# Moving the next expert's token features into the last chunk of the current expert, and reading w2 two consecutive rows to a partition

## The chip, the core and the metric

The kernel runs on one core of a Trainium2 chip. Its time is device microseconds for one execution, the median over several runs. The engines are called as in the profile: PE is TensorE (matmuls and transposes; PEld is its weight load, which overlaps), DVE is VectorE, ACT is ScalarE, POOL is GpSimd, SP is SyncE, which here only issues DMAs.

## What is computed

One block of a transformer on 1024 tokens of width 1024: a token mixer (neighbourhood attention beside a recurrent scan), a layer norm, and then a mixture of 16 experts in which every expert chooses its own 128 tokens. The change touches the experts alone:

```python
aff = softmax(u @ w_router)                      # u: (1024, 1024)
gate, idx = top_k(aff.T, cap)                    # cap = 128 tokens for each of 16 experts
xs = u[idx]                                      # (16, 128, 1024)
hdn = silu(xs @ w1) * (xs @ w3)                  # w1, w3: (16, 1024, 2816)
ye = hdn @ w2 * gate                             # w2: (16, 2816, 1024)
out = zeros.at[idx].add(ye)
```

All of it is float32.

## The kernel before, in words

The mixer takes the first half of the execution, up to about 1628 us; the experts follow, and a last layer norm ends it. The change leaves the mixer's code and the order of its instructions as they are.

**An expert.** Its 2816 hidden columns are cut in three chunks of 1024, 1024 and 768. The steps of the program are written in this order: for each expert e and chunk ci a step (e,ci,1) for w1, a step (e,ci,3) for w3, and then the w2 step of the chunk before it, which for chunk 0 is chunk 2 of expert e-1. A step is cut in units of 256 weight rows: four for w1 or w3, and four, four or three for w2. An expert has 35 units, and this text writes c0w3.1 for chunk 0, w3, unit 1.

**A unit.** `load` asks SP for it 12 units ahead (1 MB, or 768 KB for w1 and w3 of the last chunk; 13 buffers). `split`, two units ahead, makes two float32r halves of it: ACT casts (`hi`, L881), DVE subtracts (`lo`, L882). They share a ring of three buffers each, so `hi` of a unit starts when PE is done with the unit three before it. For each 128 rows PE then runs a pair of matmuls with hi·xh, a pair with lo·xh and a pair with hi·xl, where xh and xl are the halves of the tokens: at L983 into `ph` for w1 and w3, at L998 into `ye` for w2, where the halves of the hidden values (dh, dl) stand for xh and xl.

**Between the steps.** After a w1 step ACT makes silu into `hd` (L986); after w3 DVE multiplies (L988). `hd` is then transposed on PE by 128 columns at a time (L1020) into PSUM tiles named `pt`, from which ACT makes `dh` (L1021) and DVE `dl` (L1022). After the last w2 step of an expert DVE scales `ye` by gate and channel into `yo` (L1003, SCALAR_TENSOR_TENSOR), and POOL scatters it.

**The next expert's tokens.** `prep(e)` makes a one-hot matrix on DVE (L826, 8 instructions), 16 one-column matmuls on PE (L830) into a `pt`, the index of each token on DVE (CAST, L832), and a gather on POOL (L834). `prep2` then makes the features: eight transposes on PE (L846) into two `pt`, eight scale-and-shift copies out of them, four on ACT (L850) and four on DVE (L849), into a tile that is also named `yo`, and from this ACT makes xh (L852, two halves) and DVE xl (L853). `pt` has two buffers, for `prep`, `prep2` and the transposes of `hd` together:

```python
pt=ps_t.tile([128,4,128],F32,name="pt")                     # in prep2, and again for hd
if last and m==1 and ci==1 and e+1<NE: P[e+1]=prep(e+1)
if last and m==2 and ci==0 and e+1<NE: prep2(P[e+1])
```

A scheduler turns this program into one list of instructions for each engine, which the engine runs in order. It may set instructions elsewhere than where the program has them: before the change, from the fourth expert's features on, the eight transposes of `prep2` stand on PE after the last w2 unit of chunk 1, straight ahead of the six transposes of chunk 2's `hd`. The first experts have them earlier.

Of the kernel before, what the change touches and what calls it, by code (L numbers as in the profile page):

```python
# [12 lines left out]
F32 = mybir.dt.float32  # L13
F32R = mybir.dt.float32r
BF16 = mybir.dt.bfloat16
I32 = mybir.dt.int32
# [6 lines left out]
D=1024; T=1024; TC=256; TS=1280; NCT=4  # L23
# [10 lines left out]
NE=16; DE=2816; CAP=128; NT=8  # L34
# [701 lines left out]
def moe(ctx, tc, K, get_t1, mc, i, G, out):  # L736
    nc=tc.nc
    ident,mh,sc2p,sh2=G["ident"],G["mh"],G["sc2p"],G["sh2"]
# [17 lines left out]
    def behind(a,b):  # L756

        tc.add_manual_dep(b.ins,a.ins.name,mybir.DependencyInfo(mybir.DependencyClass.NoSync,mybir.DependencyReason.DATA),reason="order")
# [7 lines left out]
    with ExitStack() as c1:  # L766
        p=c1.enter_context(tc.tile_pool(name="m1",bufs=2,side="right"))
# [5 lines left out]
        for t in range(NT):  # L773
            r=slice(t*128,(t+1)*128)
# [9 lines left out]
            for hh in range(2):  # L784
                pt=ps_t.tile([128,4,128],F32,name="pt")
# [16 lines left out]
            e=p.tile([128,NE],F32,name="ex")  # L802
# [13 lines left out]
    ep=ctx.enter_context(tc.tile_pool(name="ep",bufs=2))  # L816
# [4 lines left out]
    NC_=len(FC)  # L821

    def prep(e):
        oh=ep.tile([128,NT,128],BF16,name="oh",bufs=1)
        for t in range(NT):
            oi=nc.vector.tensor_scalar(oh[:,t,:],iota,slotT[:,t,e:e+1],None,op0=ALU.is_equal)  # L826
            if e in (1,2): behind(P[0]["xi"],oi)
        pi=ps_t.tile([128,4,128],F32,name="pt")
        for t in range(NT):
            for j in range(2): nc.tensor.matmul(pi[:,0,:1],oh[:,t,:],tok[:,t,j:j+1],start=(t+j==0),stop=(t+j==NT))  # L830
        idx=ep.tile([128,1],I32,name="idx")
        ic=nc.vector.tensor_copy(idx,pi[:,0,:1])  # L832
        g=ep.tile([128,D+NE],F32,name="gath",bufs=1)
        gi=nc.gpsimd.indirect_dma_start(out=g,out_offset=None,in_=table[:,:],  # L834
            in_offset=bass.IndirectOffsetOnAxis(ap=idx[:,:1],axis=0))
        return dict(gi=gi,ic=ic,idx=idx,g=g,e=e)

    def prep2(d):
        g=d["g"]; d["gate"]=V[:,0,d["e"]:d["e"]+1]; nc.gpsimd.tensor_copy(d["gate"],g[:,D+d["e"]:D+d["e"]+1])
        xh=ep.tile([128,8,128],F32R,name="xh"); xl=ep.tile([128,8,128],F32R,name="xl")  # L840
        xf=ep.tile([128,8,128],F32,name="yo",bufs=1)
        for hh in range(2):
            pt=ps_t.tile([128,4,128],F32,name="pt")
            for k in range(4):
                kk=hh*4+k
                nc.tensor.transpose(pt[:,k,:],g[:,kk*128:(kk+1)*128],ident)  # L846
            for k in range(4):
                kk=hh*4+k
                if k%2: nc.vector.tensor_scalar(xf[:,kk,:],pt[:,k,:],sc2p[:,kk:kk+1],sh2[:,kk:kk+1],op0=ALU.mult,op1=ALU.add)  # L849
                else: nc.scalar.activation(xf[:,kk,:],pt[:,k,:],AF.Identity,bias=sh2[:,kk:kk+1],scale=sc2p[:,kk:kk+1])  # L850
            c=slice(hh*4,hh*4+4)
            nc.scalar.copy(xh[:,c],xf[:,c])  # L852
            d["xi"]=nc.vector.tensor_sub(xl[:,c],xf[:,c],xh[:,c].bitcast(F32))  # L853
        d["xh"],d["xl"]=xh,xl


    steps=[]
# [8 lines left out]
    def load(u,after=None):  # L866
        z,q=U[u]; e,ci,m=steps[z]; f0,fw=FC[ci]
        if m==2: ap,w=w2[e,f0+q*256:f0+q*256+256,:],D
        else: ap,w=(w1 if m==1 else w3)[e,q*256:q*256+256,f0:f0+fw],fw
        j=len(RN)%(RAW0+RAWB+RAW2); RN.append(0)  # L870
        z=G["raw0"] if j<RAW0 and u<len(U)-FS+LD else raw if j<RAW0+RAWB else raw2
        if len(RN)==1: r=G["r0"]
        else:
            r=z.tile([128,2048],F32,name="raw")
            di=(nc.gpsimd if after else nc.sync).dma_start(r[:,:2*w].rearrange("p (n w) -> p n w",n=2),ap.rearrange("(k p) f -> p k f",p=128))
            if after: behind(after,di)
        SP[u]=(r,w)
    def split(u):
# [6 lines left out]
    with tc.tile_pool(name="m2",bufs=2,side="right") as p:  # L885
# [34 lines left out]
        w=lambda n: p.tile([128,2,128],F32,name=n,bufs=1)  # L920
# [16 lines left out]
        P={0:prep(0)}  # L937
# [5 lines left out]
    def scale_shift(x,nm,rs,op):  # L943
        nc.vector.scalar_tensor_tensor(x,x,nm,g2row,op0=op,op1=ALU.mult)
        nc.vector.scalar_tensor_tensor(x,x,rs,b2row,op0=ALU.mult,op1=ALU.add)
# [25 lines left out]
    for u,(s,q) in enumerate(U):  # L971
        e,ci,m=steps[s]; last=q==nu(ci,m)-1
        for n in range(SN,min(u+LA+1,len(U))): split(n); SN=n+1
        if u+LD<len(U): load(u+LD)
        d=P[e]; w=SP.pop(u); f0,fw=FC[ci]; nf=fw//128
        if m!=2:
            if q==0: PH[m]=[ps_h.tile([128,512],F32,name=f"ph{m}{j}") for j,_ in halves(fw)]
            xh,xl=d["xh"],d["xl"]
            for k in (2*q,2*q+1):
                wh,wl=w[k%2]  # L980
                for x,y,a,b in ((xh,wh,True,False),(xh,wl,False,False),(xl,wh,False,True)):
                    for j,c in halves(fw):
                        nc.tensor.matmul(PH[m][j][:,:c.stop-c.start],x[:,k,:],y[:,c],start=(k==0 and a),stop=(k==7 and b))  # L983
            if last and m==1:
                hd=ep.tile([128,1024],F32,name="hd",bufs=1)
                for j,c in halves(fw): nc.scalar.activation(hd[:,c],PH[1][j][:,:c.stop-c.start],AF.Silu)  # L986
            elif last:
                for j,c in halves(fw): nc.vector.tensor_mul(hd[:,c],hd[:,c],PH[3][j][:,:c.stop-c.start])  # L988
                HD[e,ci]=hd
        else:  # L990
            if ci==0 and q==0: YE[e]=[ps_y.tile([128,512],F32,name=f"ye{j}") for j in range(2)]
            ye=YE[e]; dh,dl=DH[e,ci]
            for k in (2*q,2*q+1):
                st=(ci==0 and k==0); sp=(ci==NC_-1 and k==nf-1)
                wh,wl=w[k%2]
                for l,rr,a,b in ((dh,wh,True,False),(dh,wl,False,False),(dl,wh,False,True)):
                    for j in range(2):
                        nc.tensor.matmul(ye[j],l[:,k,:],rr[:,j*512:(j+1)*512],start=st and a,stop=sp and b)  # L998
            if ci==NC_-1 and last:
                yo=ep.tile([128,D],F32,name="yo",bufs=1)  # L1000
                for j in range(2):
                    c=slice(j*512,(j+1)*512)
                    nc.vector.scalar_tensor_tensor(yo[:,c],ye[j],d["gate"],gt2row[:,c],op0=ALU.mult,op1=ALU.mult)  # L1003
                if e<NE-1:
                    nc.gpsimd.indirect_dma_start(out=acc[:,:],out_offset=bass.IndirectOffsetOnAxis(ap=d["idx"][:,:1],axis=0),  # L1005
                        in_=yo,in_offset=None,compute_op=ALU.add)
                else:
                    nc.vector.tensor_add(yo,yo,ag);
                    nm,rs=ln_stats(nc,None,yo,mh,at=Q[:,0,:16])
                    scale_shift(yo,nm,rs,ALU.subtract)  # L1010

        nxt=steps[s+1] if s+1<len(steps) else None
        for key in list(HD) if last else ():
            if m==2 or (m==3 and (nxt is None or nxt[2]!=2)) or (nxt==(key[0],key[1],2)):
                ee,cc=key; fw2=FC[cc][1]; nf2=fw2//128
                hd=HD.pop(key)
                dh=ep.tile([128,8,128],F32R,name="dh",bufs=1); dl=ep.tile([128,8,128],F32R,name="dl",bufs=1)
                for k0 in range(0,nf2,4):
                    n=min(4,nf2-k0); ks=slice(k0,k0+n); pt=ps_t.tile([128,4,128],F32,name="pt")
                    for k in range(n): nc.tensor.transpose(pt[:,k,:],hd[:,(k0+k)*128:(k0+k+1)*128],ident)  # L1020
                    nc.scalar.copy(dh[:,ks],pt[:,:n])  # L1021
                    nc.vector.tensor_sub(dl[:,ks],pt[:,:n],dh[:,ks].bitcast(F32))  # L1022
                DH[key]=(dh,dl)
        if last and m==1 and ci==1 and e+1<NE: P[e+1]=prep(e+1)
        if last and m==2 and ci==0 and e+1<NE: prep2(P[e+1])
        if u==len(U)-FS:
            ag=ep.tile([128,D+NE],F32,name="gath",bufs=1)[:,:D]
            nc.gpsimd.indirect_dma_start(out=ag,out_offset=None,in_=acc[:,:],in_offset=bass.IndirectOffsetOnAxis(ap=P[NE-1]["idx"][:,:1],axis=0))
            gb=G["raw0"].tile([128,2048],F32,name="raw"); g2row,b2row=gb[:,:D],gb[:,D:]
            for z,n in ((g2row,2),(b2row,3)): nc.sync.dma_start(z,i["lnrows"][n:n+1,:].to_broadcast([128,D]))  # L1030
        for t in range(NT):
            if u==len(U)-XE[t]: final(t)
# [35 lines left out]
```

## Time and profile before

| what | value |
|---|---|
| median of three runs | 3291.5 us (3291.21 to 3293.4) |
| the profiled execution's own time | 3290.45 us |
| its span, first to last instruction | 3288.7 us |
| PE busy / DVE busy / ACT busy / POOL busy | 91% / 72% / 53% / 18% |
| mean granted clock of PE | 0.943 |

The span is 1.75 us under the execution's own time, and that is 1.05 us under the median. Busy shares are means over a mixer and sixteen experts whose limits differ; what the change is worth is read from the experts alone. [...]

### The profile page before, as it was taken

To read this page: it belongs to the slowest core of one execution; us is meant where nothing else is said; L and a number is where in the kernel's file an instruction comes from. 1 tells how busy PE (TensorE), PEld (TensorE's weight loads), DVE (VectorE), ACT (ScalarE), POOL (GpSimd) and SP (SyncE) were. 2 spreads that over 40 slices of the span, in tenths; PEclk is the share of its full clock that TensorE was granted. 3 is DMA by queue.
4 is the path that set the end of the run, shared out by engine and by line. 5 is a ranking of instruction groups with operands and counts; after the bars stand their busy time and mean duration, and the time that the engine had idled before them with its cause. 6 is when DMAs were issued, how large, how long until landed. Compare 5 with 4: busy or idle time off the path is not lost.

```text
span 3288.7 us, 47329 instructions
## 1 busy us (share of the span) xinstructions
PE 3007.9 (91%) x17884; PEld 2392.4 (73%) x17884; DVE 2364.2 (72%) x3206; ACT 1733.2 (53%) x1996; POOL 590.6 (18%) x509
## 2 busy tenths in 40 slices
PE   7999998997888988999699999999999999999995
PEld 4777776776667764677388887787777787777874
DVE  4346445544377678667788998888888988888887
ACT  3343343433134334332277776677666766667665
POOL 2233333333132137120000000000000000000004
PEclk9998999997889989999799999999999999999998
DMA  5345554555777866453789999999999999999975
GB/s 188 90 121 135 126 133 115 136 145 122 170 185 197 195 180 195 136 162 141 275 329 373 370 378 367 346 361 343 341 364 352 365 331 336 359 351 367 335 293 225
DMA packets 537368, 825.17 MB, mean 251 GB/s; under 512 B 206318, under 2 KB 335470, under 8 KB 537012
## 3 DMA queue, kind: packets, MB, share of 16 engines
q1 hardware_dynamic: 489308, 742.36, 66.2%
q10 hardware_dynamic: 42472, 60.25, 5.7%
q0 software_dynamic: 5360, 19.54, 2.3%
q8 instruction: 141, 2.31, 0.3%
q14 instruction: 87, 0.71, 0.1%
HBM read 732.48 MB, written 89.55 MB: 250 GB/s over the span
## 4 chain that ended last, share of the span: by engine, by line
PE 55%; DVE 6%; DMA 5%; ACT 2%; issue 2%; POOL 1%; ACTq 0%; SPq 0%; POOLq 0%; DVEq 0%
PE ph L983 29%; PE ye L998 13%; PE pA L679 3%; PE po L722 2%; DVE lo L882 2%; DMA raw<-in_w_e_dram 2%; PE pt L1020 1%; PE apt L576 1%; PE yp L583 1%; ACT hi L881 1%; PE RY L511 1%; PE RY L508 1%; PE RY L535 1%; PE US L520 1%; DMA vb<-vnD 0%
## 5 line engine op out<-in xcount | busy, mean ns | idle before, releaser
L882 DVE TENSOR_TENSOR lo<-raw,hi 128x2048 fp32r<-128x2048 f32 (+1 forms) x560 | 1199.8, 2170 | 219.4 <-ACT hi L881 202.9
L881 ACT CAST hi<-raw 128x2048 fp32r<-128x2048 f32 (+1 forms) x560 | 1009.8, 1812 | 362.0 <-PE ph L983 228.9
L983 PE MATMUL ph<-hi,xh 128*128 128x512 f32 (+1 forms) x1536 | 460.4, 384 | 3.1 <-ACT xh L852 2.0
L983 PE MATMUL ph<-lo,xh 128*128 128x512 f32 (+1 forms) x1536 | 456.6, 379 | 6.1 <-DVE lo L882 4.6
L983 PE MATMUL ph<-hi,xl 128*128 128x512 f32 (+1 forms) x1536 | 455.4, 378 | 0.4 <-DVE xl L853 0.4
L983 PEld LDWEIGHTS ph<-lo,xh 128*128 128x128 f32 x1536 | 276.6, 192 | 62.1 <-DVE lo L882 6.3
L983 PEld LDWEIGHTS ph<-hi,xh 128*128 128x128 f32 x1536 | 275.8, 193 | 54.8 <-ACT xh L852 2.4
L983 PEld LDWEIGHTS ph<-hi,xl 128*128 128x128 f32 x1536 | 274.4, 191 | 54.0 <-DVE xl L853 1.1
L228 PE MATMUL pp<-uh,whi 128*128 128x512 f32 (+1 forms) x832 | 264.3, 390 | 4.9 <-DVE th L304 3.1
L228 PE MATMUL pp<-ul,whi 128*128 128x512 f32 (+1 forms) x832 | 264.8, 387 | 0.0
L228 PE MATMUL pp<-uh,wlo 128*128 128x512 f32 (+1 forms) x832 | 262.5, 386 | 0.2 <-POOL wlo L216 0.2
L998 PE MATMUL ye<-hi,dh 128*128 128x512 f32 x704 | 221.1, 395 | 1.3 <-ACT dh L1021 1.3
L998 PE MATMUL ye<-lo,dh 128*128 128x512 f32 x704 | 220.7, 395 | 1.7 <-DVE affW L955 1.0
L998 PE MATMUL ye<-hi,dl 128*128 128x512 f32 x704 | 218.4, 391 | 3.2 <-DVE dl L1022 3.2
L1005 POOL DMA_INDIRECT acc<-yo,idx x15 | 24.1, 1604 | 951.8 <-DVE yo L1003 951.8
L228 PEld LDWEIGHTS pp<-uh,whi 128*128 128x128 f32 x832 | 153.5, 195 | 41.2 <-issue 8.2
L228 PEld LDWEIGHTS pp<-uh,wlo 128*128 128x128 f32 x832 | 155.1, 194 | 37.2 <-issue 7.5
L228 PEld LDWEIGHTS pp<-ul,whi 128*128 128x128 f32 x832 | 154.7, 194 | 36.2 <-issue 8.5
L262 DVE TENSOR_TENSOR tmp<-AU,W 120x144 f32<-120x144 f32 (+24 forms) x248 | 93.0, 375 | 116.2 <-DMA AU<-aD 50.1
L998 PEld LDWEIGHTS ye<-hi,dl 128*128 128x128 f32 x704 | 132.6, 188 | 32.3 <-DVE dl L1022 3.6
L998 PEld LDWEIGHTS ye<-lo,dh 128*128 128x128 f32 x704 | 129.3, 188 | 33.9 <-DVE lo L882 8.0
L216 POOL TENSOR_TENSOR wlo<-wraw,whi 128x512 fp32r<-128x512 f32 x86 | 113.3, 1337 | 222.0 <-ACT whi L215 170.8
(331 smaller groups left out, 4480.8 us busy)
## 6 DMA issues: line engine op xcount, KB each, us to landing
raw<-in_w_e_dram SPq DMA_DIRECT2D x430, 1024.0 KB
raw<-in_w_e_dram SPq DMA_DIRECT2D x128, 768.0 KB
wraw<-in_w_in_dram SPq DMA_DIRECT2D x86, 256.0 KB
wmod<-in_w_mod_dram SPq DMA_DIRECT2D x48, 256.0 KB
BTD<-BT SPq DMA_DIRECT2D x40, 256.0 KB
cBT<-BTD SPq DMA_DIRECT2D x40, 256.0 KB
wmod<-in_w_mod_dram SPq DMA_DIRECT2D x8, 1024.0 KB
XD<-X SPq DMA_DIRECT2D x32, 256.0 KB
```

The costliest lines, as they stand in the source:

```text
L216: nc.gpsimd.tensor_sub(l[:,ks],r,h[:,ks].bitcast(F32))
L228: nc.tensor.matmul(p,wt[:,k,:],ut[:,k,a:a+b],start=(k==0 and first),stop=(k==7 and last))
L262: nc.vector.tensor_tensor(v,AU[d][:,:,s,ts_][:,:,None,:].to_broadcast([120,2,nj,L]), W[d][:,:,js,s:s+1].to_broadcast([120,2,nj,L]),op=ALU. ...
L508: nc.tensor.matmul(RY[:M,ct*128:(ct+1)*128],X[:,ct,:M],S[d][:,ct].rearrange("p a b -> p (a b)"), start=(ct==0),stop=False,skip_group_check ...
L511: nc.tensor.matmul(RY[0:64,hd*64:(hd+1)*64],AQ[:,hd,0:64],UV[:,hd*64:(hd+1)*64], start=(first and hd==0),stop=True,skip_group_check=True)
L520: nc.tensor.matmul(US[h,ct*64:(ct+1)*64],WT[h,ct,:],R[h,ct,:],start=True,stop=True)
L679: nc.tensor.matmul(pq[q],w[:,kk,:],y[:,kk,q*512:(q+1)*512],start=(kk==0 and first),stop=(kk==3 and last))
L722: nc.tensor.matmul(pq[q],a[:,r],w[:,q*512:(q+1)*512],start=(k==0 and first),stop=(k==7 and last))
L881: nc.scalar.copy(hi[:,:2*w],r[:,:2*w])
L882: li=nc.vector.tensor_sub(lo[:,:2*w],r[:,:2*w],hi[:,:2*w].bitcast(F32))
L983: nc.tensor.matmul(PH[m][j][:,:c.stop-c.start],x[:,k,:],y[:,c],start=(k==0 and a),stop=(k==7 and b))
L998: nc.tensor.matmul(ye[j],l[:,k,:],rr[:,j*512:(j+1)*512],start=st and a,stop=sp and b)
```

## The change

Three edits. `prep` of the next expert is called after the w1 step of chunk 0, no longer chunk 1, and its index tile has three buffers. `prep2` is called in two halves, inside the w1 and the w3 step of chunk 2 (at the second unit), no longer after the w2 step of chunk 0. And a unit of w2 gives each partition two consecutive rows (one run of 8 KB) in place of two rows 128 apart (two runs of 4 KB); so that the rows meet the right hidden values, the transposes of `hd` read every second column of 256.

```diff
-        idx=ep.tile([128,1],I32,name="idx")
+        idx=ep.tile([128,1],I32,name="idx",bufs=3)
...
-    def prep2(d):
-        g=d["g"]; d["gate"]=V[:,0,d["e"]:d["e"]+1]; nc.gpsimd.tensor_copy(d["gate"],g[:,D+d["e"]:D+d["e"]+1])
-        xh=ep.tile([128,8,128],F32R,name="xh"); xl=ep.tile([128,8,128],F32R,name="xl")
-        xf=ep.tile([128,8,128],F32,name="yo",bufs=1)
-        for hh in range(2):
+    def prep2(d,hs=(0,1)):
+
+        g=d["g"]
+        if 0 in hs:
+            d["gate"]=V[:,0,d["e"]:d["e"]+1]; nc.gpsimd.tensor_copy(d["gate"],g[:,D+d["e"]:D+d["e"]+1])
+            d["xh"],d["xl"]=[ep.tile([128,8,128],F32R,name=n) for n in ("xh","xl")]
+            d["xf"]=ep.tile([128,8,128],F32,name="yo",bufs=1)
+        xh,xl,xf=d["xh"],d["xl"],d["xf"]
+        for hh in hs:
...
-            di=(nc.gpsimd if after else nc.sync).dma_start(r[:,:2*w].rearrange("p (n w) -> p n w",n=2),ap.rearrange("(k p) f -> p k f",p=128))
+            di=(nc.gpsimd if after else nc.sync).dma_start(r[:,:2*w].rearrange("p (n w) -> p n w",n=2),
+                ap.rearrange("(p k) f -> p k f" if m==2 else "(k p) f -> p k f",p=128))
...
-                    for k in range(n): nc.tensor.transpose(pt[:,k,:],hd[:,(k0+k)*128:(k0+k+1)*128],ident)
+                    for k in range(n): nc.tensor.transpose(pt[:,k,:],hd[:,(k0+k)//2*256+k%2:(k0+k)//2*256+256:2],ident)
...
-        if last and m==1 and ci==1 and e+1<NE: P[e+1]=prep(e+1)
-        if last and m==2 and ci==0 and e+1<NE: prep2(P[e+1])
+        if last and m==1 and ci==0 and e+1<NE: P[e+1]=prep(e+1)
+        if q==1 and m!=2 and ci==NC_-1 and e+1<NE: prep2(P[e+1],(m//2,))
```

Lines behind `split` move down by five (L882 is L887 after the change), those inside `prep2` by four (L846 is L850).

**Where the instructions stand.** On PE, at the end of the seventh expert (e=6) before the change, the eight transposes of `prep2` and the six of chunk 2's `hd` stand between the last w2 unit of chunk 1 and the first w1 unit of the next expert:

```order
L998 MATMUL ye_19978<-hi,dl 128x512
L998 MATMUL ye_19979<-hi,dl 128x512
L846 MATMUL pt<-ident,gath 128x128 x8
L1020 MATMUL pt<-ident,hd 128x128 x6
L983 MATMUL ph_20333<-hi,xh 128x512
```

After the change the same eight transposes stand between units c2w1.1 and c2w1.2 of that expert, both halves together:

```order
L988 MATMUL ph_20068<-hi,xl 128x512
L988 MATMUL ph_20069<-hi,xl 128x256
L850 MATMUL pt<-ident,gath 128x128 x8
L988 MATMUL ph_20068<-hi,xh 128x512
L988 MATMUL ph_20069<-hi,xh 128x256
```

The six transposes of `hd` now stand seven units behind them, after the first pair of unit c1w2.1 (a pair is two matmuls with the same halves).

On DVE the copies out of these transposes have moved with them. From unit c2w1.2 of e=6 on, after the change (each `lo` is a unit):

```order
L887 TENSOR_TENSOR lo<-raw,hi 128x1536 x2
L853 TENSOR_SCALAR yo<-pt,sc2p,sh_13371 128x128 x2
L887 TENSOR_TENSOR lo<-raw,hi 128x1536
L853 TENSOR_SCALAR yo<-pt,sc2p,sh_13371 128x128 x2
L887 TENSOR_TENSOR lo<-raw,hi 128x1536
L857 TENSOR_TENSOR xl<-yo,xh 128x512 x2
```

The next row is `lo` of c2w3.2: both `xl` stand straight ahead of it.

On DVE from unit c1w2.1 of e=6 into chunk 0 of e=7, before the change, the same copies stood between the `lo` of the next expert's first units, c0w1.0 to c0w1.3 (the first row's last two, and the two after it):

```order
L882 TENSOR_TENSOR lo<-raw,hi 128x2048 x5
L849 TENSOR_SCALAR yo<-pt,sc2p,sh_13371 128x128 x2
L882 TENSOR_TENSOR lo<-raw,hi 128x2048
L849 TENSOR_SCALAR yo<-pt,sc2p,sh_13371 128x128 x2
L853 TENSOR_TENSOR xl<-yo,xh 128x512 x2
L1022 TENSOR_TENSOR dl<-pt,dh 128x512
L1022 TENSOR_TENSOR dl<-pt,dh 128x256
L882 TENSOR_TENSOR lo<-raw,hi 128x2048 x7
```

After the change the same stretch reads:

```order
L887 TENSOR_TENSOR lo<-raw,hi 128x2048 x5
L1027 TENSOR_TENSOR dl<-pt,dh 128x512
L1027 TENSOR_TENSOR dl<-pt,dh 128x256
L887 TENSOR_TENSOR lo<-raw,hi 128x2048
L832 CAST idx<-pt 128x1
L826 TENSOR_SCALAR oh<-iota,slotT 128x128 x3
L887 TENSOR_TENSOR lo<-raw,hi 128x2048
L826 TENSOR_SCALAR oh<-iota,slotT 128x128 x5
L887 TENSOR_TENSOR lo<-raw,hi 128x2048 x5
```

Between `lo` of c0w1.2 and of c0w1.3 there now stands the index CAST, which waits for the 16 matmuls of `prep`; PE has these after the first pair of c0w1.2. Three one-hot instructions follow it, and five more stand behind the next `lo`.

On DVE at the start of chunk 1 of e=7, before the change, the two `yo` of the expert before (L1003) stand behind `lo` of c1w1.1:

```order
L882 TENSOR_TENSOR lo<-raw,hi 128x2048 x3
L1003 SCALAR_TENSOR_TENSOR yo<-ye_19978,affV,gt2row 128x512
L1003 SCALAR_TENSOR_TENSOR yo<-ye_19979,affV,gt2row 128x512
L1022 TENSOR_TENSOR dl<-pt,dh 128x512 x2
L882 TENSOR_TENSOR lo<-raw,hi 128x2048 x2
```

After the change they stand ahead of it, with the two `dl` behind it:

```order
L887 TENSOR_TENSOR lo<-raw,hi 128x2048 x3
L1008 SCALAR_TENSOR_TENSOR yo<-ye_19978,affV,gt2row 128x512
L1008 SCALAR_TENSOR_TENSOR yo<-ye_19979,affV,gt2row 128x512
L887 TENSOR_TENSOR lo<-raw,hi 128x2048
L1027 TENSOR_TENSOR dl<-pt,dh 128x512 x2
L887 TENSOR_TENSOR lo<-raw,hi 128x2048 x7
```

The orders shown last repeat to the end of the kernel: the `xl` pair in e=3 to e=14, the CAST in e=4 to e=14, the `yo` ahead of `lo` in e=4 to e=15. The earlier experts of the changed kernel have the order that the first experts had before the change.

## Rows read from the trace of the kernel before

**Rows 1.** The page: busy times, and the chain that ended last, by line.

```profile
PE 3007.9 (91%) x17884; PEld 2392.4 (73%) x17884; DVE 2364.2 (72%) x3206; ACT 1733.2 (53%) x1996; POOL 590.6 (18%) x509
...
PE ph L983 29%; PE ye L998 13%; PE pA L679 3%; PE po L722 2%; DVE lo L882 2%; DMA raw<-in_w_e_dram 2%; PE pt L1020 1%; PE apt L576 1%; PE yp L583 1%; ACT hi L881 1%; PE RY L511 1%; PE RY L508 1%; PE RY L535 1%; PE US L520 1%; DMA vb<-vnD 0%
```

**Rows 2.** Windows: length, busy us by engine, clock, DMA share, GB/s.

```profile
1768.50:1863.70 95.20, 94.89 (x467) 78.66 (x466) 86.30 (x66) 70.61 (x53) 4.27 (x3) 1.00 0.99 375
1863.70:1958.20 94.50, 94.50 (x467) 78.78 (x466) 86.06 (x66) 70.59 (x53) 4.13 (x3) 1.00 1.00 379
1958.20:3080.50 1122.30, 1069.49 (x5128) 885.49 (x5128) 953.69 (x706) 783.99 (x583) 42.56 (x33) 0.97 0.94 350
```

**Rows 3.** Timeline of PE at two edges of these windows.

```profile
1863.72 0.38 PE L830 MATMUL pt<-tok,oh 128*128 128x1 bf16 x9
...
3080.48 0.38 PE L830 MATMUL pt<-tok,oh 128*128 128x1 bf16 x9
```

**Rows 4.** Waits, 1700 to 3200 us: engine, releaser, total, times, longest.

```profile
PE pt L1020 <- DVE yo L849: 57.2, 12, 5.0
...
ACT hi L881 <- DMA raw<-in_w_e_dram: 12.1, 17, 1.1
```

**Rows 5.** Timeline, 2117 to 2124 us, all engines, some rows left out.

```profile
2117.13 1.04 PE L846 MATMUL pt<-ident,gath 128*128 128x128 f32 x8
...
2118.76 0.72 DVE L849 TENSOR_SCALAR yo<-pt,sc2p,sh 128x128 f32<-128x128 f32 x2
...
2120.49 2.29 DVE L882 TENSOR_TENSOR lo<-raw,hi 128x2048 fp32r<-128x2048 f32 x1 [1.01 <-ACT hi L881]
2122.70 0.72 DVE L849 TENSOR_SCALAR yo<-pt,sc2p,sh 128x128 f32<-128x128 f32 x2
...
2123.15 1.54 PE L1020 MATMUL pt<-ident,hd 128*128 128x128 f32 x6 [4.98 <-DVE yo L849]
```

**Rows 6.** Timeline of PE at the shortest of these waits.

```profile
2222.86 0.96 PE L1020 MATMUL pt<-ident,hd 128*128 128x128 f32 x6 [2.71 <-DVE yo L849]
```

**Rows 7.** Windows after these two waits, and one near the experts' end.

```profile
2123.20:2127.90 4.70, 4.70 (x14) 3.94 (x15) 2.44 (x5) 1.93 (x4) 0.00 (x0) 0.50 1.03 422
2223.50:2227.00 3.50, 3.11 (x10) 2.02 (x8) 3.50 (x4) 1.24 (x3) 0.00 (x0) 0.51 1.04 417
...
3218.00:3232.00 14.00, 9.46 (x48) 7.01 (x46) 9.80 (x12) 9.78 (x11) 8.69 (x4) 1.00 1.03 420
```

**Rows 8.** Timeline of PE and ACT in units of full size without waits.

```profile
1835.59 0.61 PE L983 MATMUL ph<-hi,xh 128*128 128x512 f32 x2
1835.78 1.91 ACT L881 CAST hi<-raw 128x2048 fp32r<-128x2048 f32 x1 [0.81 <-PE ph L983]
1836.04 0.62 PE L983 MATMUL ph<-lo,xh 128*128 128x512 f32 x2
...
1838.31 0.61 PE L983 MATMUL ph<-hi,xh 128*128 128x512 f32 x2
```

**Rows 9.** DVE by shape, 1863.7 to 1958.2: busy, mean ns, idle before.

```profile
L882 DVE TENSOR_TENSOR lo<-raw,hi 128x2048 fp32r<-128x2048 f32 x29 | 65.2, 2285 | 4.4 <-ACT hi L881 4.3
...
L1022 DVE TENSOR_TENSOR dl<-pt,dh 128x512 fp32r<-128x512 f32 x5 | 3.2, 683 | 0.0
...
L826 DVE TENSOR_SCALAR oh<-iota,slotT 128x128 bf16<-128x128 f32 x8 | 1.6, 279 | 0.0
...
L1003 DVE SCALAR_TENSOR_TENSOR yo<-ye,affV,gt2row 128x512 f32<-128x512 f32 x2 | 1.4, 742 | 0.0
L853 DVE TENSOR_TENSOR xl<-yo,xh 128x512 fp32r<-128x512 f32 x2 | 1.3, 683 | 0.0
```

**Rows 10.** Timeline of PE: a wait in an early expert, one near the end.

```profile
1816.17 0.73 PE L998 MATMUL ye<-lo,dh 128*128 128x512 f32 x2 [0.30 <-DVE lo L882]
...
3227.93 0.62 PE L983 MATMUL ph<-lo,xh 128*128 128x512 f32 x2 [1.50 <-DVE affW L955]
```

**Rows 11.** Instructions of L1020, 1700 to 3200 us: ns min/median/max, first and last.

```profile
L1020 PEld LDWEIGHTS pt<-ident,hd x322: 137/140/231, 1723.6 to 3175.0; 128*128 128x128 f32 x161
```

More of the change, by code (lines that the diff above doesn't have):

```diff
@@ L853, in prep2 @@
             d["xi"]=nc.vector.tensor_sub(xl[:,c],xf[:,c],xh[:,c].bitcast(F32))
-        d["xh"],d["xl"]=xh,xl
     steps=[]
```

## The prediction

> **What bounds the kernel now.** I read the page first. PE is busy 91% of the span, and the chain that ended last runs through the matmuls at L983 and L998, with the casts and the loads far behind [rows 1]. So an edit is worth what it takes from, or adds to, PE's time in the experts.
>
> The windows then cut the experts by period. An expert's `prep` matmuls (L830) recur once a period and mark its edges [rows 3]. The experts that start at 1768.5 and 1863.7 us take 95.20 and 94.50 us, with PE busy throughout and a granted clock of 1.00. The next eleven, up to 3080.5, take 1122.30, which is 102.03 each, with PE busy 1069.49 of it and a clock of 0.97 [rows 2]. Something costs each of them over 7 us.
>
> The waits name it: PE waits 57.2 us in 12 waits at the transposes of `hd` for the copies at L849, and nothing else in the experts holds PE for long [rows 4]. The timeline shows one of them. PE finishes the eight transposes of `prep2` (they start at 2117.13) and comes at once to those of `hd`, which need a `pt` buffer; both are still full. The copies that empty them share DVE with `lo`: two at 2118.76, then a `lo` of 2.29 us, then the last two at 2122.70, and PE goes on at 2123.15 after 4.98 us [rows 5]. In the two experts without a loss, the same eight transposes stood in chunk 2, apart from those of `hd`.
>
> [...]
>
> **What the stalls are worth.** Eleven periods at the mean of the two good ones, 94.85, would take 1043.35; 1122.30 less this is 78.95. The twelfth stall lies past 3080.5; at the mean of these eleven it is 7.2. Together 86.1 us. [...]
>
> **The change part by part.**
>
> *The move of prep2.* After the change the eight transposes stand between c2w1.1 and c2w1.2 in every expert, and the next user of `pt`, the `hd` transposes, comes seven units later. A unit of full size takes 2.72 us (1835.59 to 1838.31) [rows 8], while the copies were through within 6.3 us of the first transpose in the worst case above (2117.13 to 2123.42) [rows 5]. The buffers are empty in time, and nothing is late in the stall's place on PE: -86.1. The transposes themselves, 1.04 us, are as many as before. That the two halves come out together, and not one in w1 and one in w3, does not matter to this.
>
> *What the new order on DVE costs.* DVE is busy 86.06 of a good expert's 94.50 [rows 2], so only 8.4 us are free, and it runs strictly in order: what stands ahead of a `lo` and waits or works delays PE when it uses up the lead. The lead follows from the rhythm: ACT starts `hi` 0.19 us into the unit two ahead of its use and takes 1.91; `lo` takes 2.29 [rows 8, 9]; PE wants it 0.45 after its unit starts, when the first pair has been issued [rows 8]. That is 2 × 2.72 + 0.45 - 0.19 - 1.91 - 2.29 = 1.5 us to spare at most. Three places in the changed order take more.
>
> (A) The index CAST ahead of `lo` of c0w1.3. It waits for the matmuls of `prep`, which follow the first pair of c0w1.2. Counted from that unit's start: 0.45 for the pair, 16 matmuls at 0.38 for nine make 0.68 [rows 3], and for the CAST of one column I take 0.2, between nothing and a one-hot's 0.28: 1.33. Three one-hots, at a busy time of 1.6 for eight [rows 9], bring 1.93, `lo` 4.22. PE wants it at 0.68 + 2.72 + 0.45 = 3.85 and waits 0.37. Five more one-hots (1.0) and a `lo` end at 7.51; wanted at 3.85 + 0.37 + 2.72 = 6.94, a wait of 0.57. Together I take 1.0, in 11 experts.
>
> (B) Both `xl` ahead of `lo` of c2w3.2. In an early expert, where a `lo` stood between them, this stretch ended in a PE wait of 0.30 [rows 10]. One `xl` more ahead is 0.68 [rows 9]: a wait of 0.98, of which 0.30 is in the good periods already. So 0.68 in 12 experts.
>
> (C) The two `yo` of the expert before, now ahead of `lo` of c1w1.1. They need the last `ye` and start, as `hi` does behind PE, about 0.2 into unit c1w1.0. Behind them stands `lo`, and behind that the `dl` and all later `lo`. Two at 0.74 and a `lo` end at 3.97; PE wants it at 2.72 + 0.45 = 3.17 and waits 0.80. Two `dl` (1.37) and the next `lo` end at 7.63; wanted at 3.17 + 0.80 + 2.72 = 6.69, a wait of 0.94. Run back to back these instructions overlap a little, so I take 1.5 for both, in 12 experts.
>
> Sum: 11 × 1.0 + 12 × 0.68 + 12 × 1.5 = 37.2 us. The bounds: nothing, if the lead is greater than this arithmetic has it, and about 1.5 times as much, 56, if each place also delays the `hi` behind it on ACT. The two `hd` products that now stand one `lo` earlier cost about 1 us of DVE, which the eight `hd` transposes behind them (1.04 us of PE without a need for `lo`) give back: nothing; without that cover it would be another half of a microsecond twice an expert, within the bound.
>
> *Do the new waits lower the clock?* Near the end of the experts PE pauses up to 1.50 us [rows 10], in a window in which it is busy 9.46 of 14.00 us, and the clock stays 1.00 [rows 7]; behind 2.71 us it fell. All the new waits are below 1 us. I take nothing; the other end is a rival below.
>
> *w2 in 8 KB runs.* The same bytes through the same queue. All the time that `hi` waits for a load in the experts is 12.1 us, in 17 waits of at most 1.1 [rows 4], and ACT is off the path. So at most 12 us could be gained; I take 0.
>
> *hd read with a stride of two* (352 weight loads). The trace has no strided one. A straight one takes 140 ns at the median [rows 11]. Bounds: 0, and one load more for each, 352 × 0.137 = 48 us. I take 0, because PEld's work lies beside PE's and is less of it (78.78 against 94.50 us in a good expert [rows 2]), so that a somewhat longer load still fits. [...]
>
> *prep one chunk earlier, a third index buffer.* POOL gathers earlier; no engine waited for the gather on PE's path. 0.
>
> **Sum.** The profiled execution took 3290.45 us, 1.05 under the median, within what runs differ by. 3290.45 - 86.1 + 37.2 = 3241.5 us. I say 3241.
>
> **The rivals.**
>
> *The new waits are absorbed.* The stalls go and nothing replaces them: 3290.45 - 86.1 = 3204. For it: the first experts have nearly the same work and lose 0.3. Against it: their order lacks A and C. Between this and the forecast lie cases with a part of the 37.
>
> *The loads become the bound.* An expert moves 379 × 94.5 us = 35.8 MB. In the stalled stretch the queues ran at 350 GB/s with a share of 0.94, or 372 at full share; at that an expert takes 96.2 us [rows 2]. That is below 94.85 + 3.2 = 98.0, the forecast's period, so it binds only if the DVE waits are absorbed, at 3204 + 12 × 1.4 = 3221. [...] I give it one chance in twenty.
>
> *Strided weights cost.* In part, or the whole 48: up to 3290.
>
> *The clock falls behind the new waits (the other side).* [...] For it: the clock did fall behind 2.71 us. Against: it didn't behind 1.50 [rows 7].
>
> *The change does not do what it says.* It does on PE, by the order. If a copy out of `pt` were so late that the six `hd` transposes still waited, the time would stay at 3290; seven units speak against it.
>
> **How the numbers follow.** Forecast, 3222 to 3260: 50%. Absorbed, or bound by the loads at their row's rate, 3200 to 3222: 25%. Loads at 358 or a part of the strided price, 3260 to 3284: 11%. About as before (within 0.2%, 6.6 us, which is about what a measurement of this kernel can tell from no change): 5%. Slower, by the clock: 6%. Below 3200, if 8 KB runs also give something: 3%. So faster 0.89, same 0.05, slower 0.06. The range holds the first two and the lower part of the third: 3204 to 3266.
>
> **What would show it.** No wait of L1025 for L853; twelve periods near 98 us in place of 102; a clock of 1.00 through the experts; PE waiting for `lo` (L887) at L988, some six short waits an expert at c0w1.3, c0w3.0, c2w3.2, c1w1.1 and c1w1.2, 37 us in all; LDWEIGHTS of L1025 still at 140 ns. The forecast is wrong if these waits are missing (3204), if they are longer than 1.5 us or followed by the lower clock, if PE's waits come from `hi` and this from DMA, or if L1025 is slower.

## The result, and the profile after

The changed kernel takes 3240.8 us (median of 4 runs, 3235.3 to 3243.51) against 3292.45 (4 runs, 3291.21 to 3301.01): a ratio of 0.9836, interval 0.9814 to 0.9857. The forecast was 3241, the range 3204 to 3266. The profiled execution took 3235.3 us, its span is 3233.5. Runs of one kernel differ by 7 to 17 us here, much of it from the mixer: the first `hi` of the experts starts at 1586.2 us in the profiled execution of the changed kernel, at 1586.8 in that of the kernel before, and at 1587.1 to 1596.0 in four of the experiments. So the terms are compared by the experts' periods: in the changed kernel a late one, from one CAST at L832 to the next, takes 97.46 to 97.61 us.

The page of the changed kernel, busy times and the chain by line (compare [rows 1]):

```profile
PE 2999.8 (93%) x17884; PEld 2382.4 (74%) x17884; DVE 2362.5 (73%) x3206; ACT 1729.9 (53%) x1996; POOL 639.3 (20%) x509
...
PE ph L988 22%; PE ye L1003 13%; DVE lo L887 4%; PE pA L679 3%; PE po L722 2%; DMA raw<-in_w_e_dram 1%; PE pt L1025 1%; PE apt L576 1%; PE yp L583 1%; ACT hi L886 1%; PE RY L511 1%; DMA qz<-qD 1%; PE RY L508 1%; DMA bt<-in_bias_dram 1%; PE US L520 1%
```

`lo` has risen from 2% to 4% of the chain, though DVE does the same work: it is now what PE waits for. The windows of the changed kernel, two early experts and then eight late ones (columns as in [rows 2]; here an edge is the start of `hi` of an expert's c1w3.0):

```profile
1769.58:1864.90 95.32, 94.99 (x467) 79.22 (x466) 86.29 (x65) 70.63 (x53) 4.02 (x3) 1.00 0.99 374
1864.90:1960.25 95.35, 95.01 (x467) 79.21 (x466) 86.30 (x65) 70.65 (x53) 4.23 (x3) 1.00 0.99 374
2154.71:2935.07 780.36, 767.38 (x3729) 631.97 (x3728) 692.26 (x513) 567.34 (x424) 65.97 (x25) 1.00 0.97 366
```

A late period is 780.36 / 8 = 97.55 us, where it was 102 [rows 2]; the granted clock, which the profile gives as a share of full speed, is 1.00 in all three windows, where it was 0.97 in the late ones before [rows 2]. PE's waits in the changed kernel from 1700 to 3150 us (columns as in [rows 4]):

```profile
PE ph L988 <- DVE lo L887: 18.3, 55, 0.5
...
PE ye L1003 <- DVE lo L887: 1.1, 4, 0.3
```

The 57.2 us of L1020 [rows 4] are gone, no wait is over 0.54 us, and PE now waits 59 times for `lo`, where it waited twice before (0.6 us in all):

```profile
PE ye L998 <- DVE lo L882: 0.6, 2, 0.3
```

In one late expert they stand where the prediction had placed them, A, A, C, C, B. The timeline of PE in the changed kernel, its waiting instructions alone:

```profile
2418.12 0.73 PE L988 MATMUL ph<-lo,xh 128*128 128x512 f32 x2 [0.18 <-DVE lo L887]
...
2421.31 0.73 PE L988 MATMUL ph<-lo,xh 128*128 128x512 f32 x2 [0.17 <-DVE lo L887]
...
2444.74 0.74 PE L988 MATMUL ph<-lo,xh 128*128 128x512 f32 x2 [0.37 <-DVE lo L887]
...
2448.14 0.73 PE L988 MATMUL ph<-lo,xh 128*128 128x512 f32 x2 [0.34 <-DVE lo L887]
...
2490.51 0.62 PE L988 MATMUL ph<-lo,xh 128*128 128x512 f32 x2 [0.54 <-DVE lo L887]
```

Together 1.60 us an expert; what such waits cost in all is worked out below. Place A on the timeline of the changed kernel, PE and DVE:

```profile
2414.53 0.55 PE L830 MATMUL pt<-tok,oh 128*128 128x1 bf16 x16
...
2415.12 0.16 DVE L832 CAST idx<-pt 128x1 int32<-128x1 f32 x1 [1.64 <-PE pt L830]
2415.19 0.67 DVE L826 TENSOR_SCALAR oh<-iota,slotT 128x128 bf16<-128x128 f32 x3
...
2415.78 2.29 DVE L887 TENSOR_TENSOR lo<-raw,hi 128x2048 fp32r<-128x2048 f32 x1
```

DVE stands still for 1.64 us until the matmuls of `prep` are done, does three one-hots, and only then `lo`, which ends at 2418.07; PE goes on at 2418.12. Place B, ACT and DVE:

```profile
2485.39 0.87 ACT L991 ACTIVATE hd<-ph 128x512 f32<-128x512 f32 x2
...
2486.14 1.14 ACT L856 CAST xh<-yo 128x512 fp32r<-128x512 f32 x2
...
2487.17 4.67 ACT L886 CAST hi<-raw 128x1536 fp32r<-128x1536 f32 x3
2487.18 1.28 DVE L857 TENSOR_TENSOR xl<-yo,xh 128x512 fp32r<-128x512 f32 x2
...
2488.70 5.63 DVE L887 TENSOR_TENSOR lo<-raw,hi 128x1536 fp32r<-128x1536 f32 x3 [0.24 <-ACT hi L886]
```

Here the prediction blamed the two `xl`. The row of `lo` says otherwise: they are through at 2488.46, and `lo` still waits 0.24 us, for `hi`, which ACT begins only behind silu and both `xh`. The run with A, B and C put back tests this.

### The profile page after: what moved, and what is told of

Same layout as the page of the kernel before. It is cut to its first block, busy times and chain, and to the rows that moved or that the text cites. A ratio compares the mean times of both kernels' runs of the same rounds, so it can differ in the third digit from the quotient of the medians.

```text
span 3233.5 us, 47355 instructions
## 1 busy us (share of the span) xinstructions
PE 2999.8 (93%) x17884; PEld 2382.4 (74%) x17884; DVE 2362.5 (73%) x3206; ACT 1729.9 (53%) x1996; POOL 639.3 (20%) x509
## 4 chain that ended last, share of the span: by engine, by line
PE 49%; DVE 9%; DMA 5%; issue 4%; ACT 2%; POOL 1%; ACTq 0%; POOLq 0%; SPq 0%; DVEq 0%
PE ph L988 22%; PE ye L1003 13%; DVE lo L887 4%; PE pA L679 3%; PE po L722 2%; DMA raw<-in_w_e_dram 1%; PE pt L1025 1%; PE apt L576 1%; PE yp L583 1%; ACT hi L886 1%; PE RY L511 1%; DMA qz<-qD 1%; PE RY L508 1%; DMA bt<-in_bias_dram 1%; PE US L520 1%
## 5 line engine op out<-in xcount | busy, mean ns | idle before, releaser
L887 DVE TENSOR_TENSOR lo<-raw,hi 128x2048 fp32r<-128x2048 f32 (+1 forms) x560 | 1197.6, 2170 | 111.3 <-ACT hi L886 95.7
L988 PE MATMUL ph<-hi,xh 128*128 128x512 f32 (+1 forms) x1536 | 449.4, 375 | 3.1 <-ACT xh L856 2.0
L988 PE MATMUL ph<-hi,xl 128*128 128x512 f32 (+1 forms) x1536 | 448.8, 373 | 0.0
L988 PEld LDWEIGHTS ph<-lo,xh 128*128 128x128 f32 x1536 | 267.9, 189 | 95.5 <-DVE lo L887 48.4
L834 POOL DMA_INDIRECT gath<-table,idx x16 | 37.8, 2366 | 961.7 <-DVE oh L826 589.1
L1003 PE MATMUL ye<-lo,dh 128*128 128x512 f32 x704 | 223.1, 398 | 1.1 <-DVE lo L887 1.1
L1003 PE MATMUL ye<-hi,dl 128*128 128x512 f32 x704 | 219.6, 393 | 3.2 <-DVE dl L1027 3.2
L1003 PE MATMUL ye<-hi,dh 128*128 128x512 f32 x704 | 220.0, 394 | 2.5 <-ACT hi L886 1.3
L1003 PEld LDWEIGHTS ye<-hi,dl 128*128 128x128 f32 x704 | 132.9, 189 | 32.3 <-DVE dl L1027 3.6
L1003 PEld LDWEIGHTS ye<-hi,dh 128*128 128x128 f32 x704 | 131.3, 189 | 31.2 <-ACT hi L886 2.0
```

The lines of the kernel that those rows point to most:

```text
L887: li=nc.vector.tensor_sub(lo[:,:2*w],r[:,:2*w],hi[:,:2*w].bitcast(F32))
```

## The experiments

Theory 1: the gain is the collision of `prep2`'s and `hd`'s transposes that is gone, and what it leaves behind is a cost of DVE's new order at three places. Its rivals: w2's longer runs give a part; the loads bind next; the waits only move. In each diff a minus is the kernel that the run starts from. Medians of one chip session are compared with the kernel before in the same session: 3297.41 us (15 runs) for the first four, 3297.32 (9 runs) for the others.

**The w2 edit alone, on the kernel before.**

```diff
-            di=(nc.gpsimd if after else nc.sync).dma_start(r[:,:2*w].rearrange("p (n w) -> p n w",n=2),ap.rearrange("(k p) f -> p k f",p=128))
+            di=(nc.gpsimd if after else nc.sync).dma_start(r[:,:2*w].rearrange("p (n w) -> p n w",n=2),
+                ap.rearrange("(p k) f -> p k f" if m==2 else "(k p) f -> p k f",p=128))
...
-                    for k in range(n): nc.tensor.transpose(pt[:,k,:],hd[:,(k0+k)*128:(k0+k+1)*128],ident)
+                    for k in range(n): nc.tensor.transpose(pt[:,k,:],hd[:,(k0+k)//2*256+k%2:(k0+k)//2*256+256:2],ident)
```

> The kernel before with the w2 edit alone (8 KB runs, hd read with a stride of two); prep and prep2 stay where they were, and the order on DVE is that of before. Theory 1 (the gain comes from the move of prep2 alone): the twelve waits of the hd transposes for L849 stay, some 57 us in all, the late periods stay at 102.4 us, and the strided loads add about 0.2 us a period (8 transposes took 1.11 us strided and 1.04 straight), so 3 us in all: about 3294 us, a ratio of 1.001. Rival (the longer runs of w2 give a part of the gain): loads land sooner, hi waits less for them, and the time falls, by at most the 12 us of those waits: 3280 us.

3297.98 us (11 runs), ratio 1.0002, interval 0.9991 to 1.0013. The waits of this run are those of before, and eight periods (the windows have the columns of [rows 2]) take 101.95 us each:

```profile
PE pt L1021 <- DVE yo L849: 57.2, 12, 5.0
```

```profile
2164.87:2980.46 815.59, 777.08 (x3735) 644.88 (x3732) 693.62 (x513) 569.87 (x425) 29.14 (x24) 0.97 0.94 351
```

In the kernel before, the same eight periods take 815.62 us:

```profile
2162.63:2978.25 815.62, 777.50 (x3735) 643.67 (x3731) 693.43 (x513) 570.05 (x424) 31.16 (x24) 0.97 0.94 351
```

So the w2 edit by itself is worth nothing that can be measured, and the rival falls. The stride's cost is seen in the early periods, where no long wait stands. Two of them, from the first `hd` transposes of an expert's chunk 0 to those of the next expert, first in this run and then in the kernel before:

```profile
1761.67:1857.12 95.45, 95.15 (x467) 79.12 (x466) 86.31 (x65) 70.64 (x53) 4.65 (x3) 1.00 0.99 375
1857.12:1951.83 94.71, 94.71 (x468) 79.25 (x467) 86.14 (x65) 70.66 (x53) 4.06 (x3) 1.00 0.99 375
```

```profile
1759.42:1854.63 95.21, 94.91 (x467) 78.66 (x466) 86.31 (x65) 70.61 (x53) 4.33 (x3) 1.00 0.99 375
1854.63:1949.13 94.50, 94.50 (x467) 78.78 (x466) 86.06 (x65) 70.59 (x53) 4.15 (x3) 1.00 1.00 378
```

They are 0.24 and 0.21 us longer with the stride. In the late periods, where the long waits are, nothing is added; what takes it up there stays open.

**The move alone, and the stride taken out.** The first is the changed kernel without these two edits; the second keeps the 8 KB runs and takes out only the stride.

```diff
-                    for k in range(n): nc.tensor.transpose(pt[:,k,:],hd[:,(k0+k)//2*256+k%2:(k0+k)//2*256+256:2],ident)
+                    for k in range(n): nc.tensor.transpose(pt[:,k,:],hd[:,(k0+k)*128:(k0+k+1)*128],ident)
```

> The changed kernel with w2 loaded and hd read as before, so that only the move of prep and prep2 is left; the order on DVE is that of the changed kernel. Theory 1: no wait of the hd transposes, the same five short waits for lo in each late expert, LDWEIGHTS of the hd transposes back at 140 ns, a late period of 97.3 us instead of 97.55, and 3 us less than the changed kernel: about 3237 us. Rival (w2 gives a part): the gain is smaller than that of the changed kernel, 3245 us or more, and hi waits more for loads.

> The changed kernel with the 8 KB runs of w2 but hd read straight, so that hidden columns meet the wrong rows of w2: the work is the same in size, the numbers differ. Theory 1 (the stride costs about 0.2 us a period and the longer runs nothing): the same time as the run with the move alone, about 3237 us, late periods of 97.3 us, LDWEIGHTS at 140 ns. Rival (the longer runs help and the stride costs more than that): faster than the move alone by over 5 us.

The move alone takes 3238.24 us, ratio 0.9829 (0.9815 to 0.9842); without the stride it is 3238.81, 0.9826 (0.9812 to 0.9839). The whole gain is the move's (`prep` and `prep2` together; they were not moved apart). The weight loads of the `hd` transposes (ns, as in [rows 11]), first in the changed kernel, then in the one with the move alone:

```profile
L1025 PEld LDWEIGHTS pt<-ident,hd x352: 194/209/210, 1673.3 to 3189.1; 128*128 128x128 f32 x176
```

```profile
L1024 PEld LDWEIGHTS pt<-ident,hd x352: 138/140/144, 1674.3 to 3185.0; 128*128 128x128 f32 x176
```

And eight late periods each, of the move alone and of the run without the stride:

```profile
2154.45:2932.74 778.29, 765.28 (x3729) 628.82 (x3728) 692.14 (x513) 567.42 (x424) 65.96 (x25) 1.00 0.97 367
```

```profile
2163.28:2941.41 778.13, 765.29 (x3729) 628.78 (x3728) 692.15 (x513) 567.39 (x424) 65.91 (x25) 1.00 0.97 367
```

97.29 and 97.27 us: with straight reads the two layouts of w2 agree, so the longer runs give nothing. Against 97.55 the stride costs 0.27 us a period, some 4 us in all: the load takes 209 ns in place of 140, and of the 22 × 0.069 = 1.52 us that this adds up to in an expert, 0.27 shows in the period. (In the run without the stride `lo` and the waits of A, B and C are as in the changed kernel.)

**The order put back at A, B and C.** Only the order on DVE is changed; `behind(x,y)` puts y behind x and does nothing else, and LI holds the `lo` of each unit. The first line is for the one-hots in `prep`, the second for its CAST, the third for the two `yo` of L1008, the fourth and fifth for the `xl`.

```diff
+            if v: behind(v,oi)
...
+        if w: behind(w,ic)
...
+                    if u+2 in LI: behind(LI[u+2],yi)
...
+        if m==3 and ci==NC_-1 and e+1<NE and q in (1,2):
+            behind(LI[u+1],P[e+1]["x%d"%(q-1)])
-        if last and m==1 and ci==0 and e+1<NE: P[e+1]=prep(e+1)
+        if last and m==1 and ci==0 and e+1<NE: P[e+1]=prep(e+1,LI[u+2],LI.get(u-22))
```

> The changed kernel with three pieces of DVE's order put back by order-only dependencies: the index CAST behind lo of c0w3.1 and the one-hots behind lo of c1w3.1 (A), the two xl behind lo of c2w3.2 and c2w3.3 (B), the two yo behind lo of c1w1.1 (C). Theory 1 (the five short waits are due to these places): all five are gone, the late period falls from 97.55 us to that of the early experts, 95.3, and the time by 12 x 2.2 = 26 us to about 3212 us. Rival 1 (the loads bind next, at the 372 GB/s of the stalled stretch, 96.2 us a period): 3222 us, with hi waiting for loads. Rival 2 (the waits move to the next instruction, since DVE has as much to do as before): about 3238 us.

3229.32 us (5 runs), ratio 0.9799 (0.978 to 0.9818): under half of the expected gain over the changed kernel, whose interval (0.9814 to 0.9857) this one still touches, so the reading rests on the periods. Its eight late periods, and PE's waits in one of them on the timeline:

```profile
2153.63:2927.76 774.13, 763.92 (x3729) 632.87 (x3728) 691.83 (x513) 566.59 (x424) 33.16 (x25) 1.00 0.99 370
```

```profile
2348.03 0.73 PE L992 MATMUL ph<-lo,xh 128*128 128x512 f32 x2 [0.43 <-DVE lo L890]
...
2390.42 0.62 PE L992 MATMUL ph<-lo,xh 128*128 128x512 f32 x2 [0.54 <-DVE lo L890]
2395.50 0.73 PE L1007 MATMUL ye<-lo,dh 128*128 128x512 f32 x2 [0.31 <-DVE lo L890]
```

96.77 us a period: 0.78 us less than the changed kernel, where 2.25 were expected. Both waits of A are gone and one of C; the other of C is left with 0.43, since `yo` and `dl` now stand in one block. B is as long as before, 0.54, though its `xl` have moved: they weren't its cause, as the row above had said. A new wait of 0.31 has come at c1w2.0, behind the moved `xl`. So the first theory was wrong on B, and half of rival 2 came true.

**ACT's order as well.** From the run before: the two `xh` on ACT behind `hi` of c2w3.2 and c2w3.3 (HI holds the `hi`), the `xl` later and apart, the `dl` of chunk 0 two units behind the `yo`, and the one-hots one unit later than there.

```diff
-        if m==3 and ci==NC_-1 and e+1<NE and q in (1,2):
-            behind(LI[u+1],P[e+1]["x%d"%(q-1)])
+        if m==3 and ci==NC_-1 and e+1<NE:
+            if q in (1,2): behind(HI[u+1],P[e+1]["h%d"%(q-1)])
+            if q==1: behind(LI[u+2],P[e+1]["x0"])
+        if m==2 and ci==1 and e+1<NE and q==0: behind(LI[u+2],P[e+1]["x1"])
+        if m==1 and ci==1 and q==1 and e:
+            for x in DLI[-2:]: behind(LI[u+2],x)
-        if last and m==1 and ci==0 and e+1<NE: P[e+1]=prep(e+1,LI[u+2],LI.get(u-22))
+        if last and m==1 and ci==0 and e+1<NE: P[e+1]=prep(e+1,LI[u+2],LI.get(u-21))
```

> The changed kernel with DVE's and ACT's order put right at all places: A and the yo as in the run with A, B and C put back; further the two xh on ACT behind hi of c2w3.2 and c2w3.3, the xl on DVE behind lo of c2w3.3 and c1w2.2, the dl of chunk 0 behind lo of c1w1.3, the one-hots behind lo of c1w3.2. Theory (the 0.54 us at c2w3.2 come from hi, which stands behind silu and both xh on ACT, not from the xl; the 0.43 left at c1w1.2 from yo and dl in one block; each wait costs some 0.11 more than its length): no wait of PE over 0.2 us is left in a late expert, its period falls from 96.76 to 96.76 - 1.28 - 0.33 = 95.15 us, and the time from 3240.8 by 12 x 2.4 to about 3212 us. Rival 1 (the xl were the cause at c2w3.2, or the waits move on once more): the period stays above 96 us. Rival 2 (the loads bind at 372 GB/s, 96.2 us a period): 3224 us, with hi waiting for loads.

> The same with w2 loaded and hd read as before the change. Theory (the stride costs 0.28 us a period, the longer runs give nothing): a period of 94.87 us and about 3208 us. Rival (now that PE waits less, loads matter and the 8 KB runs help): slower than the run with the w2 edit, with hi waiting for loads.

3211.95 us (5 runs), ratio 0.9748 (0.9728 to 0.9768), and with the old w2 3208.62, 0.9735 (0.9713 to 0.9756). Eight late periods of the first, its waits in them, and eight of the second:

```profile
2153.27:2914.64 761.37, 759.54 (x3729) 632.63 (x3728) 691.94 (x513) 566.73 (x424) 41.26 (x25) 1.00 0.99 375
```

```profile
PE ph L992 <- DVE lo L890: 1.8, 8, 0.2
```

```profile
2153.76:2912.78 759.02, 757.20 (x3729) 629.69 (x3728) 691.52 (x513) 566.68 (x424) 41.26 (x25) 1.00 0.99 377
```

95.17 and 94.88 us a period, where 95.15 and 94.87 were expected, and one wait of 0.2 us left in each. B was ACT's: with the `xl` alone moved its wait stayed, and with the `xh` moved as well it is gone (the `xh` were not moved alone, since the `xl` read them). The loads keep up at 375 and 377 GB/s for eight experts, so they do not bind at this period. Both kernels beat the one before and the changed one. The difference between the two is 0.29 us a period, which agrees with the stride's 0.27; the intervals of their times overlap.

**One long wait in place of the short ones.** In the changed kernel the second `xl` is computed three or five times, all ahead of `lo` of c2w3.2.

```diff
-            d["xi"]=nc.vector.tensor_sub(xl[:,c],xf[:,c],xh[:,c].bitcast(F32))
+            for _ in range(3 if hh and d["e"] else 1): d["xi"]=nc.vector.tensor_sub(xl[:,c],xf[:,c],xh[:,c].bitcast(F32))
...
+            if m==3: behind(P[e+1]["xi"],LI[u+1])
```

> The changed kernel with the second xl computed three times, all ahead of lo of c2w3.2 (the same values written again), and with this the order of the early experts elsewhere, so that A and C are gone: one longer wait of PE an expert at c2w3.2, of about 0.54 + 2 x 0.68 = 1.9 us. If a wait of this length leaves the clock alone: granted clock 1.00, a period of 95.0 + 1.9 + 0.1 = 97 us. If the clock falls behind it as it did behind 2.71 us: 0.50 for some us behind it, and a period of 99.4 us.

> The same with the second xl computed five times: one wait of about 3.3 us. If the clock falls behind waits of 2.71 us and more, as before the change: 0.50 for some us behind each, about 2.35 us more than the wait, a period of 95.0 + 3.3 + 2.35 = 100.7 us. If it was something else that lowered it before the change: a clock of 1.00 and 98.4 us.

3290.13 and 3311.45 us (one run each). The 2.35 us in what was expected is an estimate: half of the 4.70 us at a clock of 0.50 behind the wait of 4.98 in the kernel before [rows 5, 7]. Neither wait is as I expected. With three `xl`, PE's waits on the timeline of two experts:

```profile
2332.81 0.73 PE L1005 MATMUL ye<-hi,dh 128*128 128x512 f32 x2 [2.26 <-ACT hi L887]
2334.86 1.01 PE L990 MATMUL ph<-lo,xh 128*128 128x512 f32 x2 [1.31 <-DVE lo L888]
...
2934.13 0.62 PE L990 MATMUL ph<-lo,xh 128*128 128x512 f32 x2 [1.67 <-DVE lo L888]
```

The windows just behind them, then seven periods that hold the first kind and three with the second:

```profile
2334.90:2340.30 5.40, 5.40 (x17) 4.63 (x18) 3.78 (x2) 1.79 (x1) 0.00 (x0) 0.50 0.84 297
2934.20:2939.60 5.40, 5.40 (x29) 4.64 (x30) 5.21 (x3) 2.87 (x3) 0.00 (x0) 1.00 1.00 379
```

```profile
2087.34:2792.63 705.29, 680.26 (x3263) 566.14 (x3262) 614.32 (x463) 494.74 (x372) 27.59 (x21) 0.97 0.97 355
2889.85:3182.64 292.79, 285.58 (x1383) 236.83 (x1382) 260.31 (x182) 212.79 (x159) 18.43 (x8) 1.00 0.97 365
```

In the first eleven experts PE has a first pair of c1w2.0 ahead and waits for its `hi`, 2.26 us, and 1.31 more right behind it; the clock is 0.50 for 5.40 us behind the one shown, and a period is 100.76 us. In the four behind them the order has no such pair, the wait is 1.67 alone, the clock stays 1.00, and a period is 97.60, C's two waits included. With five `xl` the two waits are 2.26 and 2.76 us, fourteen times each (31.6 and 38.7 us in all). The window behind one of them has the clock at 0.50 for 5.00 us, and ten periods take 102.38 us each:

```profile
2336.50:2341.50 5.00, 5.00 (x15) 4.28 (x16) 3.79 (x2) 1.38 (x1) 0.00 (x0) 0.50 0.80 278
```

```profile
2084.08:3107.87 1023.79, 973.57 (x4661) 810.80 (x4660) 890.54 (x673) 707.16 (x531) 35.88 (x30) 0.97 0.95 349
```

So a new wait at place B can be followed by the lower clock, and the rival was a real one. Behind the changed kernel's own waits, 0.54 us at most, the clock stays at 1.00 (the mean of the eight periods from 2154.71).

## Why the prediction was right, point by point

*What the stalls were worth.* Right. The period without stall, stride or wait was taken as 94.85 us; the kernel with the order mended and the old w2 measures 94.88 over eight experts. The twelve long waits (at the end of e=3 to e=14, for the features of e=4 to e=15) are gone, and so is the low clock behind them (1.00 in the eight late periods, where it was 0.97), as forecast.

*The costs of the new order.* The places were right, all three, and so were the five rows at which PE waits ("some six" waits were forecast, at five places); the size was too great. The period gives the cost: 97.55 in the changed kernel less 95.17 with the order mended is 2.38 us, where the prediction summed 1.0 + 0.68 + 1.5 = 3.18; in twelve experts that is some 29 us and not 37. The 2.38 us are also 0.8 us more than the 1.60 us that the waits show, since a row counts its wait from where the pair before it ends, 0.61 us behind that pair's start, and pairs without a wait start 0.45 behind each other [rows 8] (at B 0.51 and 0.35): 0.16 in each of the five. The term C was mis-sized most: its two waiting pairs come 0.98 and 0.96 us behind the pairs before them (2443.76 to 2444.74, 2447.18 to 2448.14), where 0.45 is usual, so that PE loses 1.0 us and not 1.5. At A the same count (2417.32 to 2418.12, 2420.52 to 2421.31) gives 0.7 and not 1.0, and at B (2489.46 to 2490.51, where 0.35 is usual) 0.7; the three make 2.4, which is what the periods say. In C the `yo` start 0.04 us behind the first pair of unit c1w1.0 (2441.04 and 2441.08), not 0.2 into it, and `lo` starts 0.08 before the second `yo` is through (2442.41 and 2442.49). The timeline of the changed kernel, DVE:

```profile
2441.08 1.41 DVE L1008 SCALAR_TENSOR_TENSOR yo<-ye,affV,gt2row 128x512 f32<-128x512 f32 x2 [1.34 <-PE ye L1003]
...
2442.41 2.28 DVE L887 TENSOR_TENSOR lo<-raw,hi 128x2048 fp32r<-128x2048 f32 x1
```

From the first `yo` to `lo` it is 1.33 us, not 1.48. In A the CAST holds DVE for 0.07 us (2415.12 to 2415.19), not 0.2. In B the step that failed is the cause: `lo` waited for `hi`, behind the two `xh` on ACT, and not for the `xl`. That the price, 0.68, came out near the 0.7 measured is luck.

*The stride.* The step "I take 0" failed. The load is half as long again, 209 ns for 140, and not hidden in full: 0.27 us a period, about 4 us. That was inside the bounds. That a longer load would still fit beside PE's work was the author's estimate: the trace of the kernel before has no strided load.

*w2 in 8 KB runs*: nothing, as forecast, both alone (815.59 us for eight periods, 815.62 without) and with PE's waits gone (95.17 us a period, 94.88 with the old w2, of which the stride is 0.27).

*The sum.* Too much for the order (some 9 us), too little for the stride (some 4), and an execution whose time varies by 8: that the median fell on the forecast is partly luck. The profiled execution, to which the sum was made, took 3235.3 against 3241.5, about what the terms are off together.

*The rivals.* Absorbed waits: refuted by the waits themselves. Loads as the bound: refuted, since with the order mended the queues moved 375 and 377 GB/s at periods of 95.17 and 94.88 us. No run shows the 358 GB/s from which the forecast takes the upper end of its range, 3266 = 3204 + 12 × 5.15, and to which its one chance in twenty was given: besides these two runs, the kernel before moved 375 and 379 GB/s over whole experts [rows 2] and 422 in a short window [rows 7]. The clock: shown to be possible, behind waits of 2.26 and 1.31 us in a row, and not met. The strided weights: in part, 4 of the 48 us.

## What to carry to other kernels

When two users of a small pool of buffers stand side by side on the engine that bounds the kernel, look at what else is queued on the engine that empties the buffers: here a `lo` of 2.29 us, itself 1.01 us late, between two pairs of copies (0.72 a pair) held PE for up to 5 us, twelve times, and the clock took about half of that again. Behind one of 4.98 us it was 0.50 for 4.70 [rows 7], and pairs of matmuls started 0.85 apart (2125.35, 2126.20, 2127.06) where 0.45 is usual [rows 8]; half of the 4.70, 2.35 us, is an estimate of what that cost. A move that takes the stall away also changes the order on the other engines; count the lead that each has and put small work where there is some, one piece at a time: here that was worth another 2.38 us in each of twelve experts, some 29 us, with no work removed. Read what ended the wait on the row of the instruction that waits, since the one that stands ahead of it may have been done long before.

## What was not expected of the hardware

A transpose whose stationary operand is read with a stride of two float32 loads in 209 ns, a straight one in 140 (medians of 352, in the changed kernel and in the one with the move alone). Behind single waits of PE of 1.67 us the granted clock stayed at 1.00; behind 2.26 and 1.31 us with one pair of matmuls between them it was 0.50 for 5.4 us. What lies between, and which of those two waits does it, was not tried.
